# The mask as an operand of the scan, the program's head laid out anew, and T3 and T4 of three quarters made at once, in a two-layer trunk on one core

## The chip, the core and the metric

The kernel runs on one core of a Trainium2 chip. The time is that of one execution of the program on the device, in microseconds (us); lower is better. The engines of the core are TensorE (PE in the profile), VectorE (DVE), ScalarE (ACT), GpSimd (POOL) and SyncE (SP), which issues the transfers. Each engine works through its own queue of instructions in order and waits there for semaphores.

## The reference, cut to what matters

Two layers over 1024 tokens of width 1024, all in float32:

```python
for l in range(DEPTH):                       # 2
    h = rms_norm(x, mix_norm_g[l])
    sb_q, sb_k, sb_v, sw_q, sw_k, sw_v, gate_logits = split(h @ w_in[l])
    o_sb  = stick_breaking_attention(sb_q, sb_k, sb_v)      # 8 heads of 64
    o_swa = sliding_window_sink_attention(rope(sw_q), rope(sw_k), sw_v, sinks[l])
    merged = gates[0] * (o_sb @ w_branch_sb[l]) + gates[1] * (o_swa @ w_branch_swa[l])
    x = x + merged @ w_out[l]
    h2 = rms_norm(x, mlp_norm_g[l])
    x = x + square(relu(h2 @ w_up[l])) @ w_down[l]          # 1024 -> 4096 -> 1024

def stick_breaking_attention(q, k, v):       # for each block of 128 queries
    z = q @ k.T * scale
    strict = s_idx < t_idx                   # only earlier tokens
    log_keep = where(strict, -softplus(z), 0)
    tail = reverse cumulative sum of log_keep, without its own term
    w = where(strict, exp(log_sigmoid(z) + tail), 0)
    return w @ v
```

So the weight of key s for query t is sigmoid(z) at s times the product of (1 - sigmoid(z)) over the keys between s and t.

## The kernel before, in words

**Products.** Every float32 product is made of three: an operand is split into a high part (a cast, on ACT) and a low part (the rest, a subtraction on DVE), both in a rounded float32 format, and `three` (L346 to L348) issues high x high, low x high and high x low. In the groups of the profile a weight has the tiles `raw` (as it arrives), `wh` and `wl`; the transposed activations are `hT`.

**Order.** A planner (class `Plan`) runs all steps as small processes with ranks and estimated costs. At each point it gives an engine the ready step of lowest rank, and the order that results is fixed as that engine's queue. `fetch` issues the transfer of a weight and then its cast and subtraction; `yield "A"`, `"D"`, `"P"`, `"G"`, `"S"` are steps on ACT, DVE, PE, POOL and SP.

**Stages.** A layer runs: `norm` of eight tiles `xt` of 128 tokens (squares and their sum on ACT L417, a reciprocal square root in small steps on ACT and DVE, the scaling to `h` on DVE L425, transposes with the identity `ident` on PE L436, eviction to `hT`); the gate products (`gates`, 16 weights `w_gate`, logits staged to DRAM) and the sliding-window branch (`swa_phase`); the stick-breaking branch (`sb_phase`); merge; output product; the feed-forward pair `up_phase` and `down_phase`.

**Stick-breaking.** A step takes one head, 128 queries and up to 512 keys (m = 128, 256, 384 or 512). Two matmuls make z in a bank of PSUM (L979, L980). Where the keys end at the queries' own block, a third, `bf16`, adds `sb_mask` to the last 128 columns (L982): a large negative number wherever the key isn't earlier. ACT makes `keep` = sigmoid(-z) (L988) and `c` = sigmoid(z) (L991). DVE runs a scan of products over `keep` from right to left (L999), with the mask's columns at 1 by then, and multiplies `c` by it (L1006). Where a query has more than 512 keys, a further step takes the product so far as the scan's initial value (`carry`, L1003). `c` is then transposed, split and multiplied with v.

**The first feed-forward product.** The tokens and the inner dimension are each cut in two, and seven products T1 to T7 in the manner of Strassen take the place of eight. Class `Quarters` makes their operands: `kept` are the transposed activations; `mixing` goes over four quarters of 128 columns and makes for each one T2 (tile `t`, `stage` before the split, L1354 and L1356), and starts `after`, which makes T3 and T4 of that quarter (L1280, in `kept`). `after` has the rank of `mixing` plus AFTER = 4000, which puts it behind other work. `up_phase` runs the products of the pairs of weights p in the order 1, 2, 6, 5, 3, 4, 7: name "6" uses `t` (T2), "5" and "3" use `quarter` and "4" and "7" use `taken`, the splits of what `after` has made (L1266 on ACT, L1269 on DVE).

## Time and profile before

| what | us |
|---|---|
| median of 3 runs (2725.91 to 2731.25) | 2726.43 |
| the profiled execution, its own time | 2727.98 |
| its span, which the rows count from zero | 2726.2 |
| PE busy in the span | 2691.2 |
| DVE busy | 1904.0 |
| ACT busy | 1402.4 |

The page gives the busy time of each engine and the chain of work that ended last. A row of the timeline gives the start of an instruction, its duration, engine, line, operation, the tiles that it writes and reads, its shape and, in brackets, how long its engine had been idle and who ended that. Rows of PE overlap: the duration includes the way through the array, and the distance from one start to the next tells what an instruction costs the queue. A row with "x8" merges eight. A view of stretches gives, for each, the busy time of the engines and the granted clock of PE as a share of full speed (1.00 is 2.4 GHz, 0.50 is 1.2 GHz).

### The profile page before, as it was taken

The numbers are of one execution on the slowest core, as the hardware profiler recorded it, in microseconds if no ns is written. First come the engines' busy times: TensorE is split into PE (matmuls) and PEld (weight loads), VectorE is DVE, ScalarE is ACT, GpSimd is POOL, SyncE is SP. The second block draws the span as 40 slices with busy tenths as digits, with TensorE's granted clock in tenths as the row PEclk, the third lists the DMA queues.
The fourth block names the chain that finished last, engine by engine and source line by source line (L and its number), as shares of the span: only waits on it lengthen the run. The fifth ranks groups of instructions, "written<-read, shape, count | busy, mean of one in ns | idle before, by whom it ended". The sixth has DMA issues, their size and how long they took to land.

```text
span 2726.2 us, 37142 instructions
## 1 busy us (share of the span) xinstructions
PE 2691.2 (99%) x13568; PEld 2280.9 (84%) x13568; DVE 1904.0 (70%) x3269; ACT 1402.4 (51%) x2777; POOL 8.9 (0%) x83
## 2 busy tenths in 40 slices
PE   7999999999999999999999999999999999999999
PEld 7888888888878888888888988888888788888887
DVE  6665888855597777767766657887646877768664
ACT  5775556643365445333457766565424644553332
POOL 0000000000000000000000000000000000000000
PEclk9999999999999999999999999999999999999999
DMA  4222221164034447996433222123530444489972
GB/s 169 82 91 71 62 62 56 52 229 164 31 120 161 142 165 265 350 375 246 160 123 94 65 63 66 58 58 97 213 147 31 147 138 160 151 318 354 339 265 88
DMA packets 159382, 411.00 MB, mean 151 GB/s; under 512 B 18656, under 2 KB 32992, under 8 KB 159200
## 3 DMA queue, kind: packets, MB, share of 16 engines
q1 hardware_dynamic: 159200, 408.63, 42.9%
q8 instruction: 107, 1.75, 0.2%
q14 instruction: 75, 0.61, 0.1%
HBM read 285.88 MB, written 114.29 MB: 147 GB/s over the span
## 4 chain that ended last, share of the span: by engine, by line
PE 95%; DVE 2%; ACT 1%; DMA 1%; issue 0%; SPq 0%; DVEq 0%; ACTq 0%
PE bank L346 28%; PE bank L347 28%; PE bank L348 27%; PE bank L1050 2%; PE bank L1083 1%; PE bank L979 1%; PE bank L980 1%; PE bank L1082 1%; PE bank L694 1%; PE bank L436 1%; PE bank L761 1%; PE bank L784 0%; PE bank L783 0%; PE bank L668 0%; PE bank L982 0%
## 5 line engine op out<-in xcount | busy, mean ns | idle before, releaser
L1266 ACT CAST operand<-dr 128x1024 fp32r<-128x1024 f32 x224 | 220.3, 1048 | 348.8 <-PE bank L348 179.1
L347 PE MATMUL bank<-operand 128*128 128x512 f32 x896 | 348.8, 389 | 0.5 <-DVE operand L1269 0.5
L346 PE MATMUL bank<-operand 128*128 128x512 f32 x896 | 348.9, 389 | 0.0
L1269 DVE TENSOR_TENSOR operand<-dr,operand 128x1024 fp32r<-128x1024 f32 x224 | 262.7, 1222 | 123.3 <-ACT operand L1266 123.0
L348 PE MATMUL bank<-operand 128*128 128x512 f32 x896 | 348.6, 389 | 0.0
L346 PE MATMUL bank<-hT,wh 128*128 128x512 f32 (+1 forms) x776 | 312.3, 402 | 0.0
L348 PE MATMUL bank<-hT,wl 128*128 128x512 f32 (+1 forms) x776 | 302.8, 390 | 0.0
L347 PE MATMUL bank<-hT,wh 128*128 128x512 f32 (+1 forms) x776 | 302.4, 390 | 0.0
L347 PEld LDWEIGHTS bank<-operand 128*128 128x128 f32 x896 | 168.2, 188 | 36.2 <-DVE operand L1269 1.4
L348 PEld LDWEIGHTS bank<-operand 128*128 128x128 f32 x896 | 168.2, 188 | 34.9
L346 PEld LDWEIGHTS bank<-operand 128*128 128x128 f32 x896 | 168.2, 188 | 34.8
L1266 ACT CAST wh<-raw 128x512 fp32r<-128x512 f32 x128 | 78.6, 614 | 187.4 <-DVE raw L1280 127.3
L348 PEld LDWEIGHTS bank<-hT,wl 128*128 128x128 f32 x776 | 146.5, 189 | 31.6
L347 PEld LDWEIGHTS bank<-hT,wh 128*128 128x128 f32 x776 | 147.2, 190 | 23.7 <-DVE hT L395 0.2
L346 PEld LDWEIGHTS bank<-hT,wh 128*128 128x128 f32 x776 | 147.3, 190 | 23.3
L332 ACT CAST wh<-raw 128x1024 fp32r<-128x1024 f32 x88 | 92.4, 1051 | 102.6 <-PE bank L348 76.6
L335 DVE TENSOR_TENSOR wl<-raw,wh 128x1024 fp32r<-128x1024 f32 x88 | 107.1, 1219 | 53.4 <-ACT wh L332 52.5
L999 DVE TENSOR_TENSOR_SCAN keep<-keep 128x128 f32<-128x128 f32 (+3 forms) x128 | 100.1, 809 | 16.2 <-ACT keep L988 16.2
L988 ACT ACTIVATE keep<-bank 128x128 f32<-128x128 f32 (+1 forms) x192 | 91.3, 499 | 38.7 <-PE bank L982 23.1
L1058 DVE TENSOR_TENSOR tl<-bank,th 128x512 fp32r<-128x512 f32 (+1 forms) x160 | 97.5, 626 | 18.2 <-ACT th L1056 16.6
L1056 ACT CAST th<-bank 128x512 fp32r<-128x512 f32 (+1 forms) x160 | 83.3, 546 | 49.2 <-PE bank L1050 46.1
L1280 DVE TENSOR_TENSOR dr<-dr 128x1024 f32<-128x1024 f32 x64 | 78.1, 1224 | 40.7 <-DMA dr<-t_scr 16.2
(201 smaller groups left out, 6592.8 us busy)
## 6 DMA issues: line engine op xcount, KB each, us to landing
dr<-in_w_down_dram SPq DMA_DIRECT2D x144, 512.0 KB, 7.7
dr<-u_scr SPq DMA_DIRECT2D x112, 512.0 KB, 6.9
u_scr<-up SPq DMA_DIRECT2D x160, 256.0 KB, 2.8
raw<-in_w_up_dram SPq DMA_DIRECT2D x68, 512.0 KB, 3.5
raw<-in_w_gate_dram SPq DMA_DIRECT2D x32, 512.0 KB, 4.2
g_scr<-stage SPq DMA_DIRECT2D x64, 256.0 KB, 2.4
gate<-g_scr SPq DMA_DIRECT2D x64, 256.0 KB, 3.0
u_scr<-stage SPq DMA_DIRECT2D x64, 256.0 KB, 4.0
```

Of the source, the lines that this page charges most:

```text
L332: nc.scalar.copy(hi[:, :n], raw[:, :n])
L335: nc.vector.tensor_tensor(lo[:, :n], raw[:, :n], f32(hi[:, :n]), ALU.subtract)
L346: nc.tensor.matmul(ps_ap, ah, bh, start=first, stop=False)
L347: nc.tensor.matmul(ps_ap, ah, bl, start=False, stop=False)
L348: nc.tensor.matmul(ps_ap, al, bh, start=False, stop=last)
L988: nc.scalar.activation(keep[:, lo:512], z, AF.Sigmoid, scale=-1.0)
L999: nc.vector.tensor_tensor_scan(later[:, ::-1], later[:, ::-1], later[:, ::-1], ini, ALU.mult, ALU.bypass)
L1056: nc.scalar.copy(th[:, :n], tr[:, :n])
L1058: nc.vector.tensor_tensor(tl[:, :n], tr[:, :n], f32(th[:, :n]), ALU.subtract)
L1266: nc.scalar.copy(op.hi(j, n), src)
L1269: nc.vector.tensor_tensor(op.lo(j, n), src, f32(op.hi(j, n)), ALU.subtract)
L1280: nc.vector.tensor_tensor(out, a, b, op)
```

## The change

There are four parts.

1. **The mask.** The 128 matmuls L982 are gone, with `sb_mask` and `ident_b`. A step that ends at the queries' own block now scans with two operands, `keep` and `begins`: state = state x keep + begins, from zero. `begins` is zero but for an identity in its last 128 columns, so the state is 0 until the column of the query itself and 1 there. The scan covers m + 1 columns. A step with a carry copies it into column 512 of its `keep` (64 copies in place of the 64 multiplications L1003) and scans m + 1 columns from 1. 64 memsets of that column on POOL go.
2. **The head.** On SP the transfers of the second `xt` and of `g` come ahead of the first gate weight. `norm` of the mixing part uses `rsqrt_short`, three steps on ACT and three on DVE. The transposes take `ident_r`, the cast identity. PE gets 104 transposes of the identity into a spare bank (`warm`), until the second tile's norm is through. The first two gate products run in pieces of 256 columns throughout (72 matmuls of 512 columns become 144 of 256). Two weights of the sliding-window branch are fetched ahead.
3. **The entry.** `after` of the first three quarters has the rank of `mixing` plus NEXT = -300.
4. **Smaller moves.** LATE_CHUNK 2, `combine` of the first pair takes its slot first, and the rings of `down_phase` hold `wh` and `wl` of a unit together.

```diff
-LATE_CHUNK = 1
+LATE_CHUNK = 2
...
-GRANK = 1.5
-W0 = 0.7
-W1 = 5.8
+GRANK = 1.2
+W0 = 1.5
+W1 = 3.5
...
+NEXT = -300
...
-    ident = cp.tile([P, P], F32, name="ident")
-    make_identity(nc, ident)
+    win_mask = cp.tile([P, 256], F32, name="win_mask")
+    make_identity(nc, win_mask[:, 0:P])
     ident_r = cp.tile([P, P], F32R, name="ident_r")
-    nc.vector.tensor_copy(ident_r, ident)
-    ident_b = cp.tile([P, P], BF16, name="ident_b")
-    nc.vector.tensor_copy(ident_b, ident)
-    sb_mask = cp.tile([P, P], BF16, name="sb_mask")
...
+    nc.vector.tensor_copy(ident_r, win_mask[:, 0:P])
+    ident = f32(ident_r)
...
+    def warm(until):
+
+        b = Bank("av")
+        yield from b.take()
+        pt = b.tile()
+        n = 0
+        while until.time is None:
+            yield "P", .5 if n < 8 else .22, 1e9
+            for _ in range(2):
+                nc.tensor.transpose(pt[:, 0:P], ident, ident)
+            n += 1
+        b.free()
...
+    def rsqrt_short(sp, y, ss):
+
+        lnv = sp.tile([P, 1], F32, tag="rs_l", name="rs_l", bufs=4)
+        a = sp.tile([P, 1], F32, tag="rs_a", name="rs_a", bufs=4)
+        yield "A", .55
+        act_set(LOGEXP)
+        nc.scalar.activation(lnv, ss, AF.Ln, scale=1.0 / D, bias=eps_t)
+        nc.scalar.activation(y, lnv, AF.Exp, scale=-0.5)
+        nc.scalar.activation(a, y, AF.Square)
+        yield "D", .15
+        nc.vector.scalar_tensor_tensor(a, ss, D * EPS, a, ALU.add, ALU.mult)
+        yield "D", .15
+        nc.vector.tensor_scalar(a, a, -0.5 / D, 1.5, ALU.mult, ALU.add)
+        yield "D", .15
+        nc.vector.tensor_tensor(y, y, a, ALU.mult)
...
-                row.append(fetch(w_swa[l, g, c], base + 500 + g * 100 + c, 768, make, wh_slots[c]))
+                if g == 0 and c < 2:
+                    row.append(ahead[c])
+                    continue
+                own = None if g else (pr_s, lambda: sw.tile([P, 4, 256], F32, tag="pr", name="raw", bufs=2).rearrange("p a b -> p (a b)"))
+                row.append(fetch(w_swa[l, g, c], base + 500 + g * 100 + c, 768, make, wh_slots[c], own=own))
...
-                n_c = 512 if l or i or half else 256
+                n_c = 512 if l or i > 1 else 256
...
-                nc.gpsimd.memset(keeps[i][:, 512:513], 1.0)
+                nc.vector.memset(keeps[i][:, 512:513], 1.0)
+
+            begins = sb.tile([P, 513], F32, name="begins")
+            nc.vector.memset(begins, 0.0)
+            nc.vector.tensor_copy(begins[:, 384:512], ident)
...
-            nc.tensor.matmul(z, qt, k2[:, c0:c1], start=False, stop=c1 != n)
-            if c1 == n:
-                nc.tensor.matmul(z[:, m - P:m], ident_b, sb_mask, start=False, stop=True)
+            nc.tensor.matmul(z, qt, k2[:, c0:c1], start=False, stop=True)
...
-            ini = 1.0
+
+            run = keep[:, lo:513][:, ::-1]
             if carry_in:
                 yield carry_in
-                ini = carry_in.value
-            yield "D", scan(m)
-            later = keep[:, lo + 1:513]
-            nc.vector.tensor_tensor_scan(later[:, ::-1], later[:, ::-1], later[:, ::-1], ini, ALU.mult, ALU.bypass)
+                first, other = carry_in.value
+                yield "D", .15
+                nc.vector.tensor_copy(keep[:, 512:513], first)
+                other.done()
+                yield "D", scan(m)
+                nc.vector.tensor_tensor_scan(run, run, run, 1.0, ALU.mult, ALU.bypass)
+            else:
+                yield "D", scan(m)
+                nc.vector.tensor_tensor_scan(run, run, begins[:, lo:513][:, ::-1], 0.0, ALU.mult, ALU.add)
...
-                nc.vector.tensor_tensor(carry, later[:, 0:1], keep[:, lo:lo + 1], ALU.mult)
...
-                yield "G", .1
-                nc.gpsimd.memset(keep[:, 512:513], 1.0)
...
-                plan.spawn(after(cs, t), self.rank + AFTER)
+                plan.spawn(after(cs, t), self.rank + (AFTER if q == 3 else NEXT))
...
+                if p == 0:
+                    yield small
+                    yield small.value[1]
...
-        a_ring = (("raw", None), ("raw", None), ("wl", 0), ("wl", 1), ("wh", 2), ("wh", 3))
-        b_ring = (("wh", 0), ("wh", 1), ("wl", 2), ("wl", 3)) + (("dr", None),) * 4 + (("late", None),) * LATE_RAWS
+        a_ring = (("raw", None), ("raw", None), ("wh", 2), ("wl", 2), ("wh", 3), ("wl", 3))
+        b_ring = (("wh", 0), ("wl", 0), ("wh", 1), ("wl", 1)) + (("dr", None),) * 4 + (("late", None),) * LATE_RAWS
...
+            if l == 0:
+                plan.spawn(warm(normed[1]), 0)
...
+            ahead = [fetch(w_swa[l, 0, c], base + 500 + c, 768, parts(c), sw_open, early=True, after=second) for c in range(2)]
```

On PE at the start of the program, before (the first tile of each name; three tiles' transposes in one row, then the first gate product):

```order
L436 MATMUL bank<-ident,h 128x128 x24
L346 MATMUL bank<-hT,wh 128x256
L347 MATMUL bank<-hT,wh 128x256
L348 MATMUL bank<-hT,wl 128x256
L346 MATMUL bank<-hT,wh 128x256
```

and now, where L359 is `warm`, L475 the transposes and L364 to L366 are `three`:

```order
L359 MATMUL bank<-ident_r 128x128 x74
L475 MATMUL bank<-ident_r,h 128x128 x8
L359 MATMUL bank<-ident_r 128x128 x14
L475 MATMUL bank<-ident_r,h 128x128 x4
L359 MATMUL bank<-ident_r 128x128 x2
L475 MATMUL bank<-ident_r,h 128x128 x4
L359 MATMUL bank<-ident_r 128x128 x14
L364 MATMUL bank<-hT,wh 128x256
L365 MATMUL bank<-hT,wh 128x256
L366 MATMUL bank<-hT,wl 128x256
```

The 74 transposes of the identity stand ahead of the first eight of `h`, and 30 more in between.

On DVE at the start, before (`xt_103` and `xt_104` are the first two tiles, L421 to L365 the small steps of the norm):

```order
L421 TENSOR_SCALAR v<-ss 128x1
L335 TENSOR_TENSOR wl<-raw,wh 128x1024
L359 TENSOR_TENSOR rs_a<-y 128x1
L361 TENSOR_TENSOR rs_a<-rs_a,v 128x1
L233 CAST ident_r<-ident 128x128
L235 CAST ident_b<-ident 128x128
L421 TENSOR_SCALAR v<-ss 128x1
L363 TENSOR_SCALAR rs_a<-rs_a 128x1
L365 TENSOR_TENSOR y<-y,rs_a 128x1
L425 SCALAR_TENSOR_TENSOR h<-xt_103,y,g 128x1024
```

and now (`xt_95` and `xt_96` are the same two tiles, L395 to L399 `rsqrt_short`):

```order
L395 SCALAR_TENSOR_TENSOR rs_a<-ss,rs_a 128x1
L397 TENSOR_SCALAR rs_a<-rs_a 128x1
L395 SCALAR_TENSOR_TENSOR rs_a<-ss,rs_a 128x1
L399 TENSOR_TENSOR y<-y,rs_a 128x1
L234 CAST ident_r<-win_mask 128x128
L397 TENSOR_SCALAR rs_a<-rs_a 128x1
L462 SCALAR_TENSOR_TENSOR h<-xt_95,y,g 128x1024
L399 TENSOR_TENSOR y<-y,rs_a 128x1
L462 SCALAR_TENSOR_TENSOR h<-xt_96,y,g 128x1024
```

The cast of `ident_r`, for which every transpose now waits, stands behind small steps of both tiles; the low part of the gate weight has moved behind the scaling of both.

On DVE at the entry of the feed-forward part of the first layer, before (L1280 makes the sums and differences, L1269 low parts, L1356 the low part of T2; the T2 of the third quarter stands five rows ahead of the first row shown, the last row is that of the fourth):

```order
L1280 TENSOR_TENSOR raw_7949<-raw_7949 128x512
L1269 TENSOR_TENSOR wh_8072<-raw_7949,wh_8072 128x512
L1269 TENSOR_TENSOR quarter_7952<-kept_7286,quarter_7952 128x512 x2
L1269 TENSOR_TENSOR wl_8073<-stage_8009,wl_8073 128x512
L1269 TENSOR_TENSOR quarter_7952<-kept_7286,quarter_7952 128x512 x2
L1269 TENSOR_TENSOR wh_8094<-raw_7949,wh_8094 128x512
L1280 TENSOR_TENSOR kept_7284<-stage_8021,kept_7284 128x4x128
L1269 TENSOR_TENSOR quarter_7953<-kept_7287,quarter_7953 128x512
L1280 TENSOR_TENSOR stage_8106<-kept_7287,kept_7286 128x512
L1269 TENSOR_TENSOR wl_8095<-raw_7980,wl_8095 128x512
L1269 TENSOR_TENSOR quarter_7953<-kept_7287,quarter_7953 128x512
L1356 TENSOR_TENSOR t2_7283<-stage_8106,t2_7283 128x4x128
```

and now, from the T2 of the third quarter to that of the fourth:

```order
L1401 TENSOR_TENSOR t2_7319<-stage_8057,t2_7319 128x4x128
L1325 TENSOR_TENSOR raw_8016<-raw_7985,raw_8016 128x512
L1325 TENSOR_TENSOR kept_7321<-kept_7321,stage_8057 128x4x128
L1325 TENSOR_TENSOR raw_7985<-stage_8045,raw_7985 128x512
L1325 TENSOR_TENSOR kept_7320<-stage_8057,kept_7320 128x4x128
L1325 TENSOR_TENSOR kept_7322<-kept_7322,kept_7320 128x4x128
L1314 TENSOR_TENSOR wh_8108<-raw_7985,wh_8108 128x512
L1325 TENSOR_TENSOR stage_8120<-kept_7323,kept_7322 128x512
L1325 TENSOR_TENSOR raw_7985<-raw_7985 128x512
L1314 TENSOR_TENSOR wl_8109<-stage_8045,wl_8109 128x512
L1401 TENSOR_TENSOR t2_7319<-stage_8120,t2_7319 128x4x128
```

Where 17 operations of DVE stood between the two (a row with x2 is two), 9 do now: the low parts of `quarter` and the weight of a later product have moved behind the fourth quarter's T2.

On PE in the stick-breaking part, before (L979 and L980 make z, L982 adds the mask):

```order
L979 MATMUL bank<-k_3015,qs 128x128
L980 MATMUL bank<-k_3016,qs 128x128
L982 LDWEIGHTS ident_b
L982 MATMUL bank<-sb_mask,ident_b 128x128
L979 MATMUL bank<-k_3015,qs 128x256
L980 MATMUL bank<-k_3016,qs 128x256
L982 LDWEIGHTS ident_b
L982 MATMUL bank<-sb_mask,ident_b 128x128
```

and now:

```order
L1026 MATMUL bank<-k_3179,qs 128x128
L1027 MATMUL bank<-k_3180,qs 128x128
L1026 MATMUL bank<-k_3179,qs 128x256
L1027 MATMUL bank<-k_3180,qs 128x256
L1026 MATMUL bank<-k_3179,qs 128x384
L1027 MATMUL bank<-k_3180,qs 128x384
```

The load of the identity and the mask's matmul are gone from between the steps, and nothing else has come there.

## Rows read from the trace of the kernel before

**Rows 1.** The page: busy us of each engine, share of the span, instructions.
```profile
PE 2691.2 (99%) x13568; PEld 2280.9 (84%) x13568; DVE 1904.0 (70%) x3269; ACT 1402.4 (51%) x2777; POOL 8.9 (0%) x83
```

**Rows 2.** Stretches (bounds, length, busy by engine, granted clock, DMA share, GB/s).
```profile
0.00:25.00 25.00, 11.83 (x65) 11.06 (x65) 16.17 (x46) 16.50 (x39) 1.87 (x11) 1.00 0.61 231
250.00:550.00 300.00, 300.00 (x1861) 261.75 (x1861) 237.17 (x398) 175.59 (x379) 3.15 (x32) 1.00 0.21 61
450.00:500.00 50.00, 50.00 (x293) 42.12 (x292) 45.96 (x79) 35.66 (x78) 0.59 (x6) 1.00 0.23 68
750.00:800.00 50.00, 43.44 (x186) 35.17 (x185) 47.40 (x85) 31.85 (x59) 0.00 (x0) 0.90 0.28 101
```

**Rows 3.** PE in order of time, 270 us: start, us, line, tiles, count.
```profile
270.48 0.23 PE L982 MATMUL bank<-sb_mask,ident_b 128*128 128x128 bf16 x1
270.52 0.36 PE L346 MATMUL bank<-wh,hT 128*128 128x256 f32 x1
270.72 0.28 PE L347 MATMUL bank<-wl,hT 128*128 128x256 f32 x1
270.84 0.28 PE L348 MATMUL bank<-wh,hT 128*128 128x256 f32 x1
...
272.21 0.23 PE L982 MATMUL bank<-sb_mask,ident_b 128*128 128x128 bf16 x1
272.28 0.50 PE L1050 MATMUL bank<-ident,c 128*128 128x128 f32 x3
```

**Rows 4.** Costliest groups of the page: busy us, mean ns, idle before.
```profile
L999 DVE TENSOR_TENSOR_SCAN keep<-keep 128x128 f32<-128x128 f32 (+3 forms) x128 | 100.1, 809 | 16.2 <-ACT keep L988 16.2
```

**Rows 5.** PE at the entry of the feed-forward part, layers 1 and 2.
```profile
769.95 0.80 PE L346 MATMUL bank<-t,wh 128*128 128x512 f32 x1 [6.20 <-ACT t L1354]
771.11 0.80 PE L347 MATMUL bank<-t,wh 128*128 128x512 f32 x1 [0.36 <-DVE t L1356]
...
781.83 0.39 PE L346 MATMUL bank<-taken,wl 128*128 128x512 f32 x1
...
789.99 0.39 PE L346 MATMUL bank<-quarter,wl 128*128 128x512 f32 x1
...
2139.74 0.39 PE L346 MATMUL bank<-quarter,wl 128*128 128x512 f32 x1
```

**Rows 6.** DVE at the same two entries.
```profile
759.53 0.69 DVE L1356 TENSOR_TENSOR t<-stage,t 128x512 fp32r<-128x512 f32 x1
...
770.36 0.69 DVE L1356 TENSOR_TENSOR t<-stage,t 128x512 fp32r<-128x512 f32 x1
...
2110.53 0.69 DVE L1356 TENSOR_TENSOR t<-stage,t 128x512 fp32r<-128x512 f32 x1
```

**Rows 7.** ACT and DVE at the head of the program.
```profile
4.61 1.06 ACT L417 ACTIVATE h<-xt 128x1024 f32<-128x1024 f32 x1 [2.60 <-DMA xt<-in_x_dram]
...
7.52 1.06 ACT L417 ACTIVATE h<-xt 128x1024 f32<-128x1024 f32 x1 [0.28 <-DMA xt<-in_x_dram]
...
8.35 0.22 DVE L233 CAST ident_r<-ident 128x128 fp32r<-128x128 f32 x1
...
9.36 1.28 DVE L425 SCALAR_TENSOR_TENSOR h<-xt,y,g 128x1024 f32<-128x1024 f32 x1 [0.25 <-DMA g<-in_g_mix_dram]
```

**Rows 8.** PE at the head of the program.
```profile
10.79 1.94 PE L436 MATMUL bank<-ident,h 128*128 128x128 f32 x8 [10.79 <-DVE rs_a L359]
...
18.70 0.56 PE L346 MATMUL bank<-hT,wh 128*128 128x256 f32 x1
...
22.47 0.28 PE L348 MATMUL bank<-hT,wl 128*128 128x256 f32 x1
...
27.69 1.06 PE L436 MATMUL bank<-ident,h 128*128 128x128 f32 x8
```

**Rows 9.** PE at 60 us, before and after the clock rises.
```profile
60.13 0.72 PE L668 MATMUL bank<-ident_r,st 128*128 128x128 f32 x4 [2.08 <-DVE st L662]
...
63.52 0.34 PE L348 MATMUL bank<-wg,hT 128*128 128x384 f32 x1
```

More of the change, by code (lines that the diff above doesn't have):

```diff
@@ L295, in stage_tile, with __init__, set @@
         return gp.tile([P, 512], F32, tag="stage", name="stage", bufs=4)
+    class Both:
+        def __init__(self, *events):
+            self.events = events
+        def set(self):
+            for e in self.events:
+                e.set()
     class Shared:
@@ L306, in done, with fetch @@
                 self.free()
-    def fetch(src, rank, n=1024, make=None, hold=None, lo_eng="D", own=None, early=False, started=None, after=None):
+    def fetch(src, rank, n=1024, make=None, hold=None, lo_eng="D", own=None, early=False, started=None, after=None, later=None):
         ev = Event(plan)
@@ L325, in go @@
                 yield hold or ring
+            if later:
+                yield later
             yield "A", act(n)
@@ L407, in halves, with norm @@
         return hs
-    def norm(npool, hslots, bufs, x_ev, g_ev, dst, t, done, ready):
+    def norm(npool, hslots, bufs, x_ev, g_ev, dst, t, done, ready, scaled=None):
         half, q = divmod(t, 4)
@@ L477, in run_group, with swa_phase @@
             three(b_tile, *w(k), *xs(k), first and k == 0, last and k == nk - 1)
-    def swa_phase(l, base, sw, swp, hT, normed, o_scr, tab_scr, finished, tail, projected):
-        wh_slots = [Slots(plan, 1) for _ in range(4)]
+    def swa_phase(l, base, ahead, sw, swp, hT, normed, o_scr, tab_scr, finished, tail, projected):
+        wh_slots = [Slots(plan, int(c > 1)) for c in range(4)]
         flight = Slots(plan, 3)
@@ L805, in swa_phase, with gates @@
                 plan.spawn(iteration(g, t), base + 1000 + (g * NT + t) * 10)
-    def gates(l, base, hT, normed, g_scr, g_ev, later, begun):
+    def gates(l, base, hT, normed, g_scr, g_ev, later, begun, head, second):
         def one(i, n):
@@ L810, in one @@
             yield gate_ring
-            ev = fetch(w_gate[l, n], base + 600 + i * .1 if l or i > 1 else (W0, W1)[i], started=begun)
+            ev = fetch(w_gate[l, n], base + 600 + i * .1 if l or i > 1 else (W0, W1)[i], started=Both(begun, second) if i == 1 else begun, later=None if l or i else head)
             yield ev
@@ L1560, in combine @@
                 r = plan.cur.rank
-                yield small.value[1]
+                if p:
+                    yield small.value[1]
                 s1 = fresh()
@@ L1913, in driver, with parts @@
             used = Event(plan, NT)
+            head = Event(plan)
+            if l == 0:
+                plan.spawn(warm(normed[1]), 0)
             for t in range(NT):
-                plan.spawn(norm(npool, hslots, 4, x_ev[t], g_ev, hT, t, used, normed[t]), base + t if l == 0 else base - 921000 + t)
+                plan.spawn(norm(npool, hslots, 4, x_ev[t], g_ev, hT, t, used, normed[t], None if l or t else head), base + t if l == 0 else base - 921000 + t)
+            second, sw_open = Event(plan), Event(plan)
+            def parts(c):
+                return lambda: [sw_open.value.tile([P, 768], F32R, tag=f"w{p}{c}", name="wg") for p in "hl"]
+            ahead = [fetch(w_swa[l, 0, c], base + 500 + c, 768, parts(c), sw_open, early=True, after=second) for c in range(2)]
             now, sb_on, sb_late = Event(plan), Event(plan), Event(plan)
@@ L1919, in driver @@
             begun = Event(plan, 16)
-            gates(l, base, hT, normed, g_scr, g_evs, [now] * EARLY + [sb_on] * (16 - EARLY - LATE) + [sb_late] * LATE, begun)
+            gates(l, base, hT, normed, g_scr, g_evs, [now] * EARLY + [sb_on] * (16 - EARLY - LATE) + [sb_late] * LATE, begun, head, second)
             yield used
@@ L1940, in driver @@
             plan.spawn(swap_right(swp, projected, q_opened), base)
-            swa_phase(l, base, sw, swp, hT, normed, o_swa, tab_scr, done, sb_on, projected)
+            swa_phase(l, base, ahead, sw, swp, hT, normed, o_swa, tab_scr, done, sb_on, projected)
             sb_phase(l, base, sb_on, opened, q_opened, hT, o_sb, sb_done, sb_late)
```

35 lines of the change are left out of this document (17 added, 18 removed).

## The prediction

> **What bounds the kernel now.** I read the busy times of the page first. PE is busy for 2691.2 of 2726.2 us [rows 1]: almost anything that makes the kernel shorter is either work taken from PE or one of the few gaps in its queue. Then the view of stretches [rows 2], for where those gaps are and which engine has room beside PE. In the 300 us from 250, which hold the stick-breaking part of layer 1, PE has no gap and DVE works 237.17 us: there only PE's own work counts, and DVE has 63 us of room, least between 450 and 500 (45.96 of 50). At the head (0 to 25) PE works 11.83 us. At the entry of the feed-forward part (750 to 800) it works 43.44 of 50 at a mean clock of 0.90, beside a DVE that works 47.40. These three places are what the change touches. The timelines of PE and DVE there [rows 3, 5 to 9] give the prices. I make the sum against the profiled execution (2727.98, of which the span is 2726.2); the median, 2726.43, is 1.55 lower, and the same difference is taken from it.
>
> **The mask: 14.7 us off PE.** The row of L982 says 0.23, but matmuls overlap, so I take distances between starts. From L982 to the next start is 0.04 (270.48 to 270.52), and the one behind takes 0.20 to its successor where its like takes 0.12 (270.52 to 270.72, 270.72 to 270.84) [rows 3]: 0.04 + 0.08 = 0.12 for each. In 13 of the 128 places transposes follow, and 0.07 is all there is to see (272.21 to 272.28). 115 x 0.12 + 13 x 0.07 = 14.7. PE has no gap in the stretch, so all of it counts. If the 0.08 stays for another reason, 128 x 0.04 = 5 is left; I find none, since in the new order the same matmuls stand next to each other.
>
> **The scan.** The trace has no scan with a second tensor. The first scans of the steps now take 809 ns in the mean, 128 of them [rows 4], and that instruction already names two operands, which are the same tile. A price of zero is nearest; one column more is a hundredth. Twice the time would be 0.81 x 64 = 52 us for each layer, inside DVE's room of 63 on paper; that is a rival below. The copies of the carry take the place of as many small multiplications, and the memsets that leave POOL waited for nobody on the ending path. No gain and no loss.
>
> **The entry: 7.1 us.** PE waits 6.20 us for T2 of the fourth quarter and 0.36 for its low part, then works at half clock for a while [rows 5]. On DVE, T2 of the third quarter starts at 759.53 and that of the fourth 18 operations later, at 770.36: 0.602 each, without a pause [rows 6]. In the new order it is 10 operations later: 765.5 instead of 770.4, so PE goes on 4.8 us sooner. But the operations that were moved are still owed. The last low part of `taken` for the first pair stands 32 operations behind T2 of the third quarter: 32 x 0.602 = 19.3, with its own 0.6 done at 779.4. 26 matmuls of the pair come behind it. 36 took from 781.83 to 789.99 [rows 5], 0.227 each, so 26 take 5.9; with 0.5 for low parts of the next product the second pair's first product starts at 785.8, 26.3 behind T2 of the third quarter, where it started at 789.99: 4.2 us gained. PE's clock hardly matters to this, since DVE ends the last waits. In layer 2 the same 26.3 behind 2110.53 [rows 6] gives 2136.8 against 2139.74 [rows 5]: 2.9. Sum 7.1. Bounds: nothing, if the new waits in the two products take everything; and 14, if the 6.56 of waiting go in both layers and half a microsecond of lost clock with each (2 x 7).
>
> **The head: 3.7 us lost.** On ACT the square of the first tile starts at 4.61 and that of the second at 7.52, behind two other transfers [rows 7]. Now the second tile comes in the second place, so ACT is done with both squares at about 7.0. Six small steps of 0.2 on ACT and five on DVE stand before the cast of `ident_r` in DVE's queue, which therefore lands at about 8.9 (it started at 8.35 before [rows 7]). Now 74 transposes of the identity must run ahead of the first real ones, which began at 10.79 and cost 0.213 each (8 in 1.94, the last one's way included) [rows 8]. At full clock they cost 0.11 (8 in 1.06 at 27.69) [rows 8]. So what counts is when the clock rises. It did so 3.8 us after the first gate product started (18.70 to 22.47) [rows 8] and 3.4 us after work resumed at 60.13, with six transposes at its start [rows 9]. I take 3.8 for transposes alone: 18 at 0.213, 56 at 0.11, end at 18.9. Behind them stand 16 real ones and 30 more of the identity, 5.1, and 0.6 of waiting for evictions: the first gate product starts at 24.6 against 18.70. Terms: 5.9 later; 0.9 for the third tile's eight transposes, done by 18.70 before and still to come now; 0.9 for 72 matmuls of 512 columns in two pieces each (2 x 0.12 - 0.227); 1.4 for more waits for `hT` between the pieces, from laying out the rows of ACT and DVE. Against that 1.9 of half clock between 18.70 and 22.47 go, and at 60 us the wait of 2.08 with the half clock behind it until 63.52 [rows 9], 3.5 together: ACT stood there behind the cast of a gate weight still in transfer, and the sliding-window weights now come sooner. 5.9 + 0.9 + 0.9 + 1.4 - 1.9 - 3.5 = 3.7. Bounds: 1 if the clock rises at once and nothing waits; 12 to 16 if it doesn't rise.
>
> **Smaller moves.** LATE_CHUNK and the rings of `down_phase` move weights between stages in which PE has no gap: nothing, with 2 us either way for the range.
>
> **Sum.** -14.7 - 7.1 + 3.7 = -18.1: 2709.9 for the profiled execution, 2708.3 from the median.
>
> **Rivals.**
> A. *Transposes don't raise the clock.* Nothing in the trace has transposes alone for long enough; 3.4 against 3.8 [rows 8, 9] speaks for counting them, thinly. Then all 120 run at 0.213: the first gate product starts at 34.8 (10.2 later) and its 3.8 at half clock, worth 1.9, come back. 2708.3 + 12.1 = 2720.4.
> The Trainium skill ("TensorE: Matmul & The Clock Gate", section "Part 4: PE-mode transpose") says that transposes don't count as busy PE in the same way and that the full clock doesn't engage for them. By that rule the result is this rival's 2720.4; the trace doesn't decide it.
> B. *The entry gives all.* If the low parts come ahead of PE's need (ACT's casts in another order, fewer operations of DVE in between), 14 in place of 7.1: 2701.4. Against it: DVE works without a pause there and the number of its operations is the same.
> C. *The scan becomes the bound; slower.* One mechanism: with a second tensor to read a scan takes twice as long. DVE's work in the 300 us becomes 289. The densest 50 us show 45.96 [rows 2], a share of 0.919; if that is as tight as DVE can be packed, the stretch takes 314.4 us, 14.4 longer in each layer, and the mask's gain is gone: 2726.43 + 28.8 - 7.1 + 3.7 = 2751.8. It turns the result slower where the stretch grows by more than 1.7 (half of 7.1 - 3.7): DVE 301.7 x 0.919 = 277.3, so 40 us more on 64 scans, from a mean of 1.44 us a scan. Against it: the two operands that the instruction has already.
> D. *It doesn't do what it says at the entry:* the new waits take the whole 7.1. 2715.4 alone, within 0.2% if A comes with it (2727.5).
>
> **How the numbers follow.** Forecast 0.72, A 0.13, B 0.06, C 0.04, D 0.05. About 0.2% (5.45 us, so 2721.0 to 2731.9) is what a measurement of this kernel can tell from no change. A lies at that bound, so half of it counts as the same, with a fifth of D and some of what I haven't seen: faster 0.72 + 0.06 + 0.06 + 0.03 = 0.87, same 0.09, slower 0.04 for C. The range goes from B less 2 us for the smaller moves, 2699, to A, 2721; that leaves out C and the tails.
>
> **What would show it.** The stick-breaking stretch of PE without a gap and 7 us shorter in each layer, first scans near 810 ns; DVE's T2 of the fourth quarter 6 us behind that of the third, PE's wait there 1.4 instead of 6.2, then several waits of half a microsecond for `quarter` and `taken`; PE starting at about 9 with transposes whose distance falls from 0.213 to 0.11 before 14, the first gate product between 24 and 26, and no wait at 60 us. A scan over 1.4 us, a distance that stays at 0.213, or a wait of PE in the stick-breaking part would prove me wrong.

## The result and the profile after

The changed kernel takes 2711.66 us (median of 4 runs, 2711.21 to 2712.77) beside 2727.14 for the kernel before on the same chip (4 runs). The ratio is 0.9938 with a 95% interval of 0.9926 to 0.9951: faster by 0.5 to 0.7%. The profiled execution took 2711.21, with a span of 2709.4; 16.8 less than the profiled execution of before, where 18.1 were forecast, and the median 2711.66 where 2708.3 were.

PE's queue gives the place of the difference. The table takes the start of the same matmul in both traces, between which PE has the same work but for what the change takes out or adds:

| from the start of the program to | before | after | shift | shift since the line above | forecast |
|---|---|---|---|---|---|
| first product with `quarter`, layer 1 (head, mask) | 750.91 | 747.15 | -3.76 | -3.76 | 3.7 - 7.35 = -3.65 |
| second pair's first product, layer 1 (entry) | 789.99 | 782.47 | -7.52 | -3.76 | -4.2 |
| first product with `quarter`, layer 2 (mask, smaller moves) | 2101.92 | 2088.17 | -13.75 | -6.23 | -7.35 |
| second pair's first product, layer 2 (entry) | 2139.74 | 2123.48 | -16.26 | -2.51 | -2.9 |
| last matmul | 2722.09 | 2705.33 | -16.76 | -0.50 | 0 |

The first line, in which the head's loss and the mask's gain stand together, comes out as forecast; each gain behind it is somewhat smaller than forecast. How much of a line belongs to which part of the change is told by the runs below.

The stretches, after (bounds, length, busy time of PE, PE's weight loads, DVE, ACT and POOL, granted clock, DMA share, GB/s), which answer to [rows 2]:

```profile
250.00:550.00 300.00, 300.00 (x1829) 267.11 (x1828) 238.91 (x407) 175.98 (x381) 0.00 (x0) 1.00 0.23 64
450.00:500.00 50.00, 50.00 (x291) 43.70 (x290) 48.69 (x83) 37.05 (x82) 0.00 (x0) 1.00 0.26 68
745.00:795.00 50.00, 47.25 (x203) 36.96 (x202) 49.00 (x88) 32.36 (x63) 0.00 (x0) 0.97 0.31 105
```

PE still has no gap in the stick-breaking part, where DVE now works 238.91 of 300 and, from 450 to 500, where it is densest, 48.69. The entry has 47.25 of 50 for PE, at a clock of 0.97. PE in order of time there, after, where [rows 3] stood before:

```profile
273.36 0.39 PE L1027 MATMUL bank<-k,qs 128*128 128x512 f32 x1
273.59 0.28 PE L364 MATMUL bank<-wh,hT 128*128 128x256 f32 x1
273.70 0.28 PE L365 MATMUL bank<-wl,hT 128*128 128x256 f32 x1
```

From the last z matmul of a step to the next product 0.23 (273.36 to 273.59), and from that one to its successor 0.11, where 0.20 stood after the mask: the removed matmul took its 0.08 along. The scans of the widest and the narrowest steps, after, and the widest of before (busy us, mean ns, idle before):

```profile
L1050 DVE TENSOR_TENSOR_SCAN keep<-keep,begins 128x513 f32<-128x513 f32 x32 | 38.5, 1204 | 0.0
L1050 DVE TENSOR_TENSOR_SCAN keep<-keep,begins 128x129 f32<-128x129 f32 x32 | 13.4, 420 | 8.7 <-ACT keep L1033 8.5
...
L999 DVE TENSOR_TENSOR_SCAN keep<-keep 128x512 f32<-128x512 f32 x32 | 38.4, 1199 | 0.0
```

The two widths between take 946 and 671 ns. The mean of the four is 0.81 us, as in [rows 4]: the second tensor costs nothing here.

The entry, PE after, which answers to [rows 5]:

```profile
761.38 0.50 PE L364 MATMUL bank<-t,wh 128*128 128x512 f32 x1 [1.38 <-ACT t L1399]
762.53 0.50 PE L365 MATMUL bank<-t,wh 128*128 128x512 f32 x1 [0.66 <-DVE t L1401]
...
773.56 0.50 PE L365 MATMUL bank<-taken,wl 128*128 128x512 f32 x1 [0.23 <-DVE taken L1314]
...
775.97 0.50 PE L365 MATMUL bank<-taken,wl 128*128 128x512 f32 x1 [0.24 <-DVE taken L1314]
...
782.47 0.39 PE L364 MATMUL bank<-quarter,wl 128*128 128x512 f32 x1
```

and DVE, which answers to [rows 6]:

```profile
755.77 0.68 DVE L1401 TENSOR_TENSOR t<-stage,t 128x512 fp32r<-128x512 f32 x1
...
761.79 0.68 DVE L1401 TENSOR_TENSOR t<-stage,t 128x512 fp32r<-128x512 f32 x1
...
775.23 0.68 DVE L1314 TENSOR_TENSOR taken<-kept,taken 128x512 fp32r<-128x512 f32 x1
```

The distance on DVE is 6.02 (10 operations of 0.602), PE's wait is 1.38 where it was 6.20, and new waits of a quarter of a microsecond stand at the low parts of `taken`. The second pair starts 26.7 behind T2 of the third quarter (755.77 to 782.47); 26.3 were forecast.

The head, PE after, which answers to [rows 8]:

```profile
8.77 9.97 PE L359 MATMUL bank<-ident_r 128*128 128x128 f32 x74 [8.77 <-DVE rs_a L397]
18.58 1.04 PE L475 MATMUL bank<-ident_r,h 128*128 128x128 f32 x8
...
23.52 0.36 PE L364 MATMUL bank<-hT,wh 128*128 128x256 f32 x1
```

with ACT's first eviction:

```profile
19.21 1.07 ACT L427 CAST hT<-bank 128x512 fp32r<-128x512 f32 x2 [7.71 <-PE bank L475]
```

and DVE's cast:

```profile
8.49 0.22 DVE L234 CAST ident_r<-win_mask 128x128 fp32r<-128x128 f32 x1
```

The 74 transposes of the identity start at 8.77, when the cast is done, and end at 18.6. ACT, which is to evict the first real ones, sits idle for 7.71 us until then. The first gate product starts at 23.52, where it started at 18.70.

### The profile page after: what moved, and what is told of

It reads as the page before. It is cut to its first block, busy times and chain, and to the rows that moved or that the text cites. A ratio compares the mean times of both kernels' runs of the same rounds, so it can differ in the third digit from the quotient of the medians.

```text
span 2709.4 us, 37024 instructions
## 1 busy us (share of the span) xinstructions
PE 2687.3 (99%) x13616; PEld 2289.6 (85%) x13616; DVE 1901.5 (70%) x3248; ACT 1404.8 (52%) x2793; POOL 2.2 (0%) x9
## 4 chain that ended last, share of the span: by engine, by line
PE 92%; DVE 4%; ACT 3%; DMA 1%; issue 1%; SPq 0%; DVEq 0%; ACTq 0%
PE bank L364 27%; PE bank L366 27%; PE bank L365 27%; PE bank L1095 2%; PE bank L1128 1%; PE bank L1026 1%; PE bank L1027 1%; PE bank L1127 1%; PE bank L737 1%; PE bank L475 1%; PE bank L804 1%; ACT pr L761 1%; ACT pr L784 0%; PE bank L827 0%; DMA raw<-in_w_gate_dram 0%
## 5 line engine op out<-in xcount | busy, mean ns | idle before, releaser
L364 PE MATMUL bank<-operand 128*128 128x512 f32 x896 | 349.1, 390 | 0.0
L366 PE MATMUL bank<-operand 128*128 128x512 f32 x896 | 348.6, 389 | 0.0
L365 PE MATMUL bank<-operand 128*128 128x512 f32 x896 | 348.6, 389 | 0.0
L364 PE MATMUL bank<-hT,wh 128*128 128x512 f32 (+1 forms) x800 | 312.7, 391 | 0.0
L366 PE MATMUL bank<-hT,wl 128*128 128x512 f32 (+1 forms) x800 | 306.3, 383 | 0.0
L365 PE MATMUL bank<-hT,wh 128*128 128x512 f32 (+1 forms) x800 | 305.6, 382 | 0.0
L366 PEld LDWEIGHTS bank<-operand 128*128 128x128 f32 x896 | 168.2, 188 | 35.0
L364 PEld LDWEIGHTS bank<-operand 128*128 128x128 f32 x896 | 168.2, 188 | 34.7
L365 PEld LDWEIGHTS bank<-operand 128*128 128x128 f32 x896 | 168.2, 188 | 34.6
L366 PEld LDWEIGHTS bank<-hT,wl 128*128 128x128 f32 x800 | 150.3, 188 | 31.1 <-DVE wl L340 0.4
L365 PEld LDWEIGHTS bank<-hT,wh 128*128 128x128 f32 x800 | 150.8, 188 | 23.1
L364 PEld LDWEIGHTS bank<-hT,wh 128*128 128x128 f32 x800 | 150.6, 188 | 23.0
L1325 DVE TENSOR_TENSOR dr<-dr 128x1024 f32<-128x1024 f32 x64 | 78.1, 1220 | 46.7 <-DMA dr<-t_scr 26.7
L1050 DVE TENSOR_TENSOR_SCAN keep<-keep,begins 128x129 f32<-128x129 f32 (+3 forms) x128 | 100.0, 810 | 8.7 <-ACT keep L1033 8.5
```

The lines of the kernel that those rows point to most:

```text
L364: nc.tensor.matmul(ps_ap, ah, bh, start=first, stop=False)
L365: nc.tensor.matmul(ps_ap, ah, bl, start=False, stop=False)
L366: nc.tensor.matmul(ps_ap, al, bh, start=False, stop=last)
L1050: nc.vector.tensor_tensor_scan(run, run, begins[:, lo:513][:, ::-1], 0.0, ALU.mult, ALU.add)
L1325: nc.vector.tensor_tensor(out, a, b, op)
```

## Experiments

All runs have 4 or 5 timed executions, each beside the kernel before on the same chip (2728.0 to 2728.3 there). A difference between two of them is given with their medians; the intervals of the ratios are 0.0013 wide to either side, and the executions of one changed kernel lie within about 2 us of each other (those of the kernel before within 7).

### The mask alone

```diff
 (the kernel before; with it the identity is made in `win_mask`, and the transposes take its cast)
...
-            if c1 == n:
-                nc.tensor.matmul(z[:, m - P:m], ident_b, sb_mask, start=False, stop=True)
+                nc.vector.tensor_tensor_scan(run, run, begins[:, lo:513][:, ::-1], 0.0, ALU.mult, ALU.add)
...
```

> The kernel before with the mask's part alone: no L982, scans with begins, the carry copied; the identity is made in win_mask so that the memory holds begins. Theory (removed matmuls are worth 0.12 each on a PE without gaps): 14.7 us below the kernel before, 2712.4 beside 2727.1. Rival (part of the 0.12 stays as distance between the z matmuls of neighbouring steps, or DVE's new order makes PE wait): 11 us or less, 2716 or more.

2712.43 us, ratio 0.9939 (0.9927 to 0.9952): 15.6 below the kernel before by the medians, 15.3 by the spans. By the marks of the table the stretch with the head and the mask of layer 1 gives 6.8 and that with the mask of layer 2 gives 7.6; the entries, whose order is as before, 0.8. The stick-breaking part by itself is seen between the last matmuls with `st`, ahead of it, and the first with `mT`, behind it; PE issues the same in between but for 64 matmuls:

| from the last `st` to the first `mT` | before | the mask alone | less |
|---|---|---|---|
| layer 1 | 232.16 to 657.83: 425.67 | 232.65 to 651.03: 418.38 | 7.29 |
| layer 2 | 1580.58 to 2008.84: 428.26 | 1572.70 to 1993.70: 421.00 | 7.26 |

That is 14.55 for 128 matmuls, 0.114 each. The layer 1 stretch of the other table gives half a microsecond less because the head of this kernel is that much later (232.65 against 232.16). The windows of this run:

```profile
250.00:550.00 300.00, 300.00 (x1830) 267.06 (x1829) 237.59 (x400) 177.76 (x382) 0.00 (x0) 1.00 0.23 66
450.00:500.00 50.00, 50.00 (x292) 43.63 (x291) 49.11 (x83) 35.47 (x77) 0.00 (x0) 1.00 0.25 69
```

PE has no gap, although DVE now works 49.11 of the densest 50 us. The theory holds. That DVE can be packed so tightly goes against a premise of rival C, which took 0.919 for the most.

### The mask and the entry, without the new head

```diff
 (the kernel with the mask alone)
-                plan.spawn(after(cs, t), self.rank + AFTER)
+                plan.spawn(after(cs, t), self.rank + (AFTER if q == 3 else NEXT))
...
             def combine():
+                if p == 0:
+                    yield small
+                    yield small.value[1]
```

> The kernel before with the mask's part and the entry's part (NEXT, and combine of the first pair taking its slot first), the head, LATE_CHUNK and the rings as before. Theory (the new head costs 3.6 us): 14.7 + 6.3 below the kernel before, 2706, faster than the changed kernel by 3 to 6 us. Rival (the head is worth nothing either way and the mask gives less): as the changed kernel, 2711.7.

2707.24 us, ratio 0.9923 (0.9909 to 0.9936): 5.2 below the mask alone and 4.4 below the whole change. (`combine`, counted among the smaller moves, is in this run.) The head and the other smaller moves together cost 4.4. In layer 2 the stretch between the entries gives 7.8 here and 6.2 in the whole change, so that 1.6 of this isn't at the head.

### The entry undone

```diff
-NEXT = -300
+NEXT = AFTER
```

> The changed kernel with T3 and T4 of all four quarters at the old rank (NEXT = AFTER). Theory (the entry is worth what the marks of the two traces say, 3.8 and 2.5): 6.3 us above the changed kernel, 2718. Rival (what is gained at the entry is given back in the rest of the first product): 2 us or less above it.

2717.84 us, 6.2 above the changed kernel. PE at the entry of layer 1:

```profile
766.85 0.80 PE L364 MATMUL bank<-t,wh 128*128 128x512 f32 x1 [6.20 <-ACT t L1399]
```

The old wait of 6.20 is back. With the run before this fixes the entry at 5.2 to 6.2 by the medians. By the marks of these runs' own traces, from the first product with `quarter` to the second pair's first product, it is 5.5 (from the mask alone to the mask and the entry: 38.36 to 35.29 and 37.77 to 35.33) and 6.1 (from this run to the whole change: 38.16 to 35.32 and 38.61 to 35.31). Nothing is given back in the rest of the product.

### No transposes of the identity

```diff
-                plan.spawn(warm(normed[1]), 0)
+                pass
```

> The changed kernel without the 104 transposes of the identity. Theory (they raise the clock, but the real transposes stand behind them for 8 us): the first real transposes at 10, the first gate product near 16 at half clock until about 20, which costs 2 us; 3 to 6 us below the changed kernel, 2707. Rival (a risen clock at the first product is worth more than the delay): 2 us above it, 2713.5.

2703.16 us (2703.05 to 2703.20), ratio 0.9906 (0.9893 to 0.9920): 8.5 below the changed kernel and the fastest of all. PE:

```profile
9.87 3.67 PE L475 MATMUL bank<-ident_r,h 128*128 128x128 f32 x16 [9.87 <-DVE h L462]
14.59 0.38 PE L364 MATMUL bank<-hT,wh 128*128 128x256 f32 x1 [1.05 <-ACT hT L427]
15.32 0.39 PE L365 MATMUL bank<-hT,wh 128*128 128x256 f32 x1 [0.34 <-DVE hT L429]
15.54 0.28 PE L366 MATMUL bank<-hT,wl 128*128 128x256 f32 x1
15.66 0.28 PE L364 MATMUL bank<-hT,wh 128*128 128x256 f32 x1
```

The real transposes start at 9.87, and the first gate product at 14.59, 8.9 sooner than in the changed kernel. The 16 transposes, one behind the other, raise the clock themselves: 3.67 for 16 is 0.22 each, and the first gate products already follow each other at 0.12 (15.54 to 15.66). I expected half clock until about 20, and that was why I put the gain at 3 to 6; the direction was right and the size too small. Without `warm`, then, the new head is better than the old one: 2703.16 against 2707.24.

### The cast of the identity first

```diff
+    with tc.manual_schedule():
-    win_mask = cp.tile([P, 256], F32, name="win_mask")
+        win_mask = cp.tile([P, 256], F32, name="win_mask")
...
-    nc.vector.tensor_copy(ident_r, win_mask[:, 0:P])
+        nc.vector.tensor_copy(ident_r, win_mask[:, 0:P])
```

> The changed kernel with the constants written in the fixed order, so that the cast of ident_r stands first in DVE's queue instead of sixth. Theory (the 74 transposes wait for that cast alone): they start at about 1.6 instead of 8.8, the clock rises at about 5, they end near 11.5 and the first gate product starts near 16.5 instead of 23.5; 4 to 6 us below the changed kernel, 2706.5. Rival (the tiles of x and the gate weights set the pace then, and PE waits for them instead): 1 us, 2710.5.

2704.25 us, 7.4 below the changed kernel with all 104 transposes in it, where 4 to 6 were expected. PE:

```profile
1.61 9.96 PE L360 MATMUL bank<-ident_r 128*128 128x128 f32 x74 [1.61 <-DVE eps_t L246]
11.41 1.04 PE L476 MATMUL bank<-ident_r,h 128*128 128x128 f32 x8
```

The same 74 transposes take the same 9.96 us, but from 1.61. The first gate product starts at 16.35. So 7.4 of the 8.5 us that the transposes cost come from their place behind the sixth instruction of DVE's queue, the cast, which stands behind steps that wait for ACT's squares.

### Only 58 of them, and those early

```diff
 (the kernel with the cast first)
-        while until.time is None:
+        while n < 29:
```

> The changed kernel with the cast of ident_r first and only 58 transposes of the identity, all ahead of the first real ones. Theory (what costs in the change is that the fillers stand in the real ones' way; a clock that has risen by then is worth having): they end at 9.7, before the first tile's h; the 16 real ones run at full clock, the first gate product starts at 13.4 instead of 14.6, 1 us below the kernel without fillers, 2702. Rival (the fillers' clock is worth nothing, since the real transposes raise it in time and the evictions set the pace): as without fillers, 2703.2, or slower.

2703.56 us (2702.77 to 2704.59): as without fillers, and the rival's way. PE:

```profile
1.61 8.47 PE L360 MATMUL bank<-ident_r 128*128 128x128 f32 x58 [1.61 <-DVE eps_t L246]
9.92 1.05 PE L476 MATMUL bank<-ident_r,h 128*128 128x128 f32 x8
11.27 1.09 PE L476 MATMUL bank<-ident_r,h 128*128 128x128 f32 x8 [0.30 <-DVE h L463]
14.65 0.39 PE L365 MATMUL bank<-hT,wh 128*128 128x256 f32 x1 [2.29 <-ACT hT L428]
```

and ACT:

```profile
10.41 1.06 ACT L452 ACTIVATE h<-xt 128x1024 f32<-128x1024 f32 x1 [2.23 <-DMA xt<-in_x_dram]
...
12.41 1.05 ACT L338 CAST wh<-raw 128x1024 fp32r<-128x1024 f32 x1
...
14.03 1.05 ACT L428 CAST hT<-bank 128x512 fp32r<-128x512 f32 x2
```

The real transposes now run at full clock and end at 12.3, 1.2 sooner, but the first gate product starts at 14.65 as it did at 14.59. ACT sets that start. It waits 2.23 for the third tile's transfer, with the eviction of the first two queued behind that square, then casts the gate weight, and comes to the second tile's eviction at 14.03. In the kernel without fillers the rows are the same:

```profile
10.32 1.06 ACT L451 ACTIVATE h<-xt 128x1024 f32<-128x1024 f32 x1 [2.16 <-DMA xt<-in_x_dram]
...
13.97 1.05 ACT L427 CAST hT<-bank 128x512 fp32r<-128x512 f32 x2
```

What fillers can win up to there is thus hidden behind ACT's order. Nor does their clock last: PE idles 2.29 us ahead of that product, and behind it the clock is at half again, which it is not in the kernel without fillers:

```profile
16.00:19.00 3.00, 3.00 (x16) 3.00 (x15) 2.83 (x6) 2.71 (x8) 0.00 (x0) 0.50 0.75 292
```

The gain forecast for this run, 1 us, didn't come.

### The gate weight's cast not held back

```diff
 (the kernel without fillers)
-            ev = fetch(w_gate[l, n], base + 600 + i * .1 if l or i > 1 else (W0, W1)[i], started=Both(begun, second) if i == 1 else begun, later=None if l or i else head)
+            ev = fetch(w_gate[l, n], base + 600 + i * .1 if l or i > 1 else (W0, W1)[i], started=Both(begun, second) if i == 1 else begun, later=None)
```

> The changed kernel without the fillers, and with the first gate weight's cast no longer held back until the first tile's h is made. In the kernel without fillers ACT waits 2.16 for the third tile (8.2 to 10.3) with the first evictions and that cast behind it, and the first gate product starts at 14.6. Theory (ACT's order sets that start): the cast runs at 9.3 in ACT's idle time; the product starts about a microsecond sooner, 1 us below, 2702. Rival (the low part of that weight now stands ahead of the second tile's h on DVE and delays its transposes by 1.2): as without the edit or 1 us above, 2704.

2703.91 us (2702.86 to 2704.32), the rival's value. The planner now puts the low part of the weight ahead of the second tile's h on DVE and three tiles' transposes ahead of the first product, and PE shows the pauses between them:

```profile
10.05 1.97 PE L475 MATMUL bank<-ident_r,h 128*128 128x128 f32 x8 [10.05 <-DVE h L462]
12.72 1.97 PE L475 MATMUL bank<-ident_r,h 128*128 128x128 f32 x8 [0.70 <-DVE h L462]
15.68 1.97 PE L475 MATMUL bank<-ident_r,h 128*128 128x128 f32 x8 [1.00 <-DVE h L462]
17.30 0.56 PE L364 MATMUL bank<-hT,wh 128*128 128x256 f32 x1
```

Each wait names DVE's h. Moving one cast moves the limit from ACT to DVE: the first gate product starts at 17.30, 2.7 later than without the edit and not 1 sooner, with eight more transposes done by then. It also runs at half clock until 20.0 (starts 0.21 apart). That the program loses only 0.75 by all this, within the spread of its executions, shows that the start of the first product alone doesn't set its time.

### The two sliding-window weights not fetched ahead

```diff
 (the kernel without fillers)
...
-                if g == 0 and c < 2:
+                if False:
...
-            ahead = [fetch(w_swa[l, 0, c], base + 500 + c, 768, parts(c), sw_open, early=True, after=second) for c in range(2)]
+            ahead = None
```

> The changed kernel without the fillers and without the two sliding-window weights fetched ahead; the rest of the new head stays. Theory (those transfers are what took the wait of 2.08 at 60 us away, with the half clock behind it): a wait of PE for st of 2 to 3 us near 55 us and half clock behind it, 3 to 4.5 us above the kernel without fillers, 2707. Rival (the wait went with the other order of the transfers or the shorter norm steps): no difference, 2703.2.

2707.25 us, 4.1 above the kernel without fillers: the theory's number, but not its mechanism. The wait for `st` comes to 0.71, not 2 to 3, and no half clock follows it:

```profile
59.15 0.51 PE L711 MATMUL bank<-ident_r,st 128*128 128x128 f32 x4 [0.71 <-DVE st L705]
```

In this execution the clock fell at the head, behind a stretch in which PE worked 1.36 of 3 us. The same fall stands in the run with LATE_CHUNK 1 (below); its row is the third:

```profile
13.50:16.50 3.00, 1.36 (x9) 1.17 (x10) 2.79 (x6) 2.94 (x9) 0.00 (x0) 1.00 1.03 410
16.70:20.00 3.30, 3.30 (x18) 3.30 (x17) 2.65 (x5) 2.61 (x7) 0.00 (x0) 0.50 0.14 53
...
16.70:20.00 3.30, 3.30 (x18) 3.30 (x17) 2.57 (x6) 2.62 (x7) 0.00 (x0) 0.50 0.38 149
```

That run reaches the first product with `quarter` of layer 1 at 739.44, 0.3 behind the kernel without fillers (739.14); this one reaches it at 742.90, 3.8 behind. So the fall costs little, and nearly all of the 4.1 goes with the late weights. Little of it is waiting: up to there PE's idle time is the same to 0.4 us in the two runs with the fall. The rest lies in longer distances between the starts of the sliding-window branch's matmuls (products of `ph` and `pl` with `vt`: 17.4 us for 60 against 14.8), and what lengthens them isn't shown.

### The pieces of the gate products as before

```diff
 (the kernel without fillers)
-                n_c = 512 if l or i > 1 else 256
+                n_c = 512 if l or i or half else 256
```

> The changed kernel without the fillers and with the gate products' pieces as before (512 columns but for the first half of the first). Theory (72 cuts cost 0.0125 each, 0.9 in all, and smaller pieces only help PE to start before the fourth tile of a half is there): between 0.9 us below the kernel without fillers and 2 above it, forecast 1 above, 2704. Rival (PE has other work meanwhile): 0.9 below, 2702.3.

2704.64 us, 1.5 above the kernel without fillers: smaller pieces are worth about 1.5 us though 72 more matmuls are issued, close to what can be told here. The forecast for this run was 1. In this trace PE works 6.55 us of the 10 from 15 to 25, and 9.25 in the kernel without fillers; of the 3.45 us without work 3.0 are two waits for DVE's h (2.25 at 21.84, 0.77 at 23.70), and the clock is at half behind them. So what the smaller pieces buy is work for PE while the later tiles' h is made.

### LATE_CHUNK back at 1

```diff
 (the kernel without fillers)
-LATE_CHUNK = 2
+LATE_CHUNK = 1
```

> The changed kernel without the fillers and with LATE_CHUNK back at 1. In layer 2, between the entry of layer 1 and that of layer 2, the changed kernel is 1.4 us worse against its own instructions than the kernel with the mask and the entry alone. Theory (the later start of the late gates packs the sliding-window and stick-breaking parts worse): 1 to 2.5 us below the kernel without fillers, 2701.5. Rival (the shorter norm steps or the weights fetched ahead do it): no difference, 2703.2.

2709.37 us, 6.2 above the kernel without fillers. My theory was wrong, in sign too. In layer 2 PE now waits, behind the stick-breaking part, for weights that ACT casts and DVE splits:

```profile
1906.54 0.50 PE L364 MATMUL bank<-op,wh 128*128 128x512 f32 x1 [0.29 <-ACT op L337]
...
1907.80 0.50 PE L365 MATMUL bank<-op,wh 128*128 128x512 f32 x1 [0.76 <-DVE op L340]
...
1909.82 0.50 PE L364 MATMUL bank<-op,wh 128*128 128x512 f32 x1 [1.28 <-ACT op L337]
...
1911.08 0.79 PE L365 MATMUL bank<-op,wh 128*128 128x512 f32 x1 [0.76 <-DVE op L340]
```

3.1 us of waits, and the clock falls behind them (0.85 in the mean from 1904 to 1914). The kernels with the head of before have LATE_CHUNK 1 without such waits there, so the value belongs with the rest of the order that the planner makes. The forecast's "nothing, with 2 us either way" for the smaller moves was thus not knowledge of the parts; where it came near, that was luck.

## Why the prediction was right, and where its steps missed

**The mask.** Right in mechanism and size. 14.7 forecast; the mask alone shortened the two stick-breaking parts by 7.29 + 7.26 = 14.55. Counting distances between starts, and not the 0.23 of the row, was what made it right: 128 x 0.23 would have been 29.

**The scan.** Right: 0.81 in the mean before and after. The argument that the old instruction already named two operands carried.

**The entry.** Right in mechanism: T2 of the fourth quarter 10 operations behind that of the third, PE's wait 1.38 (1.4 forecast), then DVE as the bound of the rest of the first pair. That PE's clock hardly matters to this is borne out: from the first product with `quarter` to the second pair's first product it is 35.32 here, with a granted clock of 0.50 from 763.5 to 766.5, and 35.32 in the run with the gate weight's cast not held back (739.52 to 774.84), whose clock there is 1.00 throughout.

Its size was too large. 26.7 instead of 26.3 behind the third quarter's T2, which is the whole of the 0.8 that is missing (6.3 instead of 7.1, 0.4 in each layer). The step that was too small is the one up to the last low part of `taken`: it starts 19.46 behind that T2 (775.23) and not 19.3, since DVE has a pause of its own in between (770.22 to 771.01 for one step, where 0.60 is usual), and PE goes on at 775.97, 20.2 behind it, where 19.9 were counted; the 26 matmuls from there on took 6.5 (775.97 to 782.47), where 5.9 and 0.5 were.

And part of the 6.3 isn't the entry's. In layer 1 of the kernel before the stretch takes 39.08, with the clock at half for some 10 us of it (0.50 from 767 to 776), but only 38.36 and 38.16 in the two runs that have the old order there and the half clock for some 7 us. Measured against those, the entry gives the 5.5 and 6.1 named above: the 7.1 was 1.0 to 1.6 too high, in part because the 789.99 that it was taken from holds that longer half clock.

**The head.** The step in most doubt, that transposes raise the clock, is shown. The stretches of the changed kernel in which PE does nothing but transposes of the identity:

```profile
9.00:12.00 3.00, 3.00 (x15) 3.00 (x15) 2.41 (x3) 1.15 (x2) 1.30 (x3) 1.00 1.02 418
12.50:15.50 3.00, 3.00 (x30) 3.00 (x28) 0.00 (x0) 0.00 (x0) 0.00 (x0) 1.00 1.03 414
```

The clock column shows no fall because the record of it begins at the first change; the counts tell the level. 15 transposes in 3 us, then 30: 0.2 each, then 0.1. The kernel with the cast first shows the same from its own start:

```profile
2.00:5.00 3.00, 3.00 (x16) 3.00 (x15) 0.00 (x0) 0.64 (x2) 0.54 (x2) 1.00 0.88 348
5.50:8.50 3.00, 3.00 (x30) 3.00 (x29) 0.64 (x5) 2.35 (x9) 0.00 (x0) 1.00 1.00 322
```

So work of this kind alone takes the clock from half to full: between 12.0 and 12.5 where it starts at 8.77, between 5.0 and 5.5 where it starts at 1.61, so 3.2 to 3.9 later; 3.8 was taken from [rows 8]. The Trainium skill ("TensorE: Matmul & The Clock Gate", section "Part 4: PE-mode transpose") says that the full clock doesn't engage for transposes. The traces differ from it: for these, float32 and one behind the other, the distance between starts fell from 0.213 to 0.109 with nothing else on PE. Rival A, which needed it to stay at 0.213, fell with that. (Its sum is slightly off as well: 102 of its 120 transposes at 0.213 in place of 0.11 are 10.5 and not 10.2, which gives 2720.7.) The cast was done at 8.7 (8.9 forecast), the 74 ended at 18.6 (18.9), the first gate product started at 23.5 (24.6). At the last matmuls with `st` in layer 1, ahead of the stick-breaking part, the changed kernel is 3.4 behind the kernel before (235.59 against 232.16). That this lies so near to 3.7 owes something to errors that cancel. The product starts 1.1 sooner than forecast, and the 1.4 for waits for `hT` between the pieces isn't there: from 23.52 to 62 PE works 38.28 of 38.48 us. Against that, small waits that the sum had at nothing came later: from 62 to 235.59 PE idles 2.1 us (171.47 of 173.59), in the kernel before from 62.20 to 232.16 0.65.

What the prediction didn't see is how good the new head is without its fillers; it priced the head only with them. Its term of 3.7 is in truth two: by the medians -4.1 for the new head without fillers, the smaller moves with it, and +8.5 for the fillers behind a late cast.

**The rest of layer 2.** 1.1 of the 1.3 that are missing in the sum are here: 6.23 against 7.35, where the mask alone gave 7.6. The loss lies between the first gate product of layer 2 and the first product with `mT`. PE's work there is the same in the changed kernel (first row) and in the one with the mask and the entry alone (second row):

```profile
1369.04:1995.09 626.05, 625.11 (x3535) 547.82 (x3533) 446.52 (x914) 380.71 (x897) 0.00 (x0) 1.00 0.30 94
1365.94:1990.39 624.45, 623.67 (x3535) 547.69 (x3534) 444.63 (x917) 381.19 (x897) 0.00 (x0) 1.00 0.30 95
```

The stretch is 1.6 longer with the new head, but PE's idle time in it is 0.9 against 0.8: the loss is hardly waiting. It is longer distances between starts while PE counts as busy, as in the run without the weights ahead (120 transposes of `pr` take 13.1 against 11.7). The sum had nothing for this. The runs without the weights ahead, with whole pieces and with LATE_CHUNK 1 don't bring it back; whether the shorter norm or the rings do it wasn't tried, and the cause stays open.

## What to carry to other kernels

Price an instruction on a full engine by the distance between its neighbours' starts with and without it, not by its own duration. Before filling an idle engine to raise its clock, look in the queue for what the filler waits for and what stands behind it: here 104 small instructions, behind a cast that stood sixth in another engine's queue, cost 8.5 us, and with the cast first 1.1. Where two engines take turns to set a start, as ACT and DVE did at the head, speeding up the one that waits for them moves nothing. And a mark of one execution holds that execution's clock: before a difference between two traces is put down to the change, compare the granted clock in both.

## What the runs showed of the hardware

Float32 transposes on PE, with nothing else beside them, raised the granted clock from 1.2 to 2.4 GHz 3.2 to 3.9 us after their start, in two runs (from 8.77 and from 1.61), and behind 16 real ones without a pause (9.87 to 13.54) the first products ran at the full one. Where the real ones came in groups of eight with PE waiting 0.70 and 1.00 us between them (the gate weight's cast not held back), the first products behind them still ran at half clock (0.21 apart from 17.66 to 20.0, then 0.12). Taking out a 128x128 bf16 matmul from between float32 ones saved 0.114 us each (14.55 for 128), half of the 0.23 that its row shows. A scan on DVE with another tensor as its second operand costs what one with the same tensor costs (1204 against 1199 ns for 513 and 512 columns).
